# Loading the value weights in the order they are written, and giving the last quarter its own buffer

## The chip, the cores and the metric

The kernel runs on one core of one Trainium2 chip. The metric is the device time of one execution in microseconds. The five engines of a core have their own instruction queues and wait for each other only by semaphores: TensorE (PE) multiplies, VectorE (DVE), ScalarE (ACT) and GpSimd (POOL) work element by element, and SyncE (SP) only issues transfers between device memory and the on-chip memory. Each queue is worked off strictly in order.

## The reference

One step of a streaming encoder layer on 1024 prompt frames and 64 sample frames of width 1024. What matters here is its beginning: every frame is normalised by its root mean square, and the normalised frames are multiplied by one wide weight matrix that makes queries, keys, values, gates and more.

```python
def rmsnorm(x, g):
    xf = x.astype(jnp.float32)
    xf = xf * lax.rsqrt(jnp.mean(xf * xf, axis=-1, keepdims=True) + EPS)
    return (xf * g.astype(jnp.float32)).astype(x.dtype)

def project(x, g_norm, w_in, b_f):
    h = rmsnorm(x, g_norm) @ w_in
    q, k, v, gf, zf, u, gp, qm, gm = jnp.split(h, IN_SPLITS, axis=-1)
    logf = jax.nn.log_sigmoid(zf + b_f)
    ...
```

After that come causal attention with forget gates over 8 heads, attention to 256 memory tokens over 4 heads, a pooling mixer, a gated output projection, and a last normalisation. All of it is computed in float32 precision.

## The kernel before

**Arithmetic.** Each float32 operand of a large product is split into a high part (rounded to the fast matmul type) and a low part (the residue). A product is three matmuls: high by high, high by low, low by high. In the traces the high parts are `xh` and `whi`, the low parts `xl` and `wlo`. A high part is made by an ACT copy (or a DVE cast), a low part by one subtraction on DVE or POOL.

**The first stage.** The frames come in three chunks, `CH` (L30): frames 0 to 255 (x0), 256 to 767 (x1), 768 to 1087 (x2, with the 64 sample frames). `load_x` (L695) loads a chunk transposed, raw in `xr`, and splits it into `xh` and `xl`. The value weights come in four raw quarters called `wr`: `wv0` holds the first 256 value columns and the 8 forget columns, in two quarters of 4 k-slices each, and `wv1` the other 256 columns, in two quarters. `load_v` (L413) loads and splits one quarter. `load_w1` (L735) does so for `wv1`. All four raw quarters go through one ring of three buffers, so the fourth takes the buffer of the first.

**The statistics.** The root mean square of a frame comes from a second load of x, by frames instead of transposed: `load_r` (L720) calls `rstd` (L438), which loads blocks of 128 frames into `nat` (a ring of three buffers of 512 KB) and sums the squares, most blocks on ACT and the second block of a chunk on DVE. In the order, `nat_15`, `nat_16`, `nat_17` belong to x2, `nat_36`, `nat_37` to x0, and `nat_50` to `nat_53` to x1. The scale is applied only when a product leaves PSUM, from a small tile `rcol`.

**The value products.** `proj_v` (L724) computes, chunk by chunk, one PSUM accumulator per 128 frames and half of the columns. There are eight PSUM banks, two each of `pp`, `s`, `pt` and `o`. An accumulator's bank is free when its product has been scaled by `rcol` and copied out (`vr`, `zt`, and `vlo` for the sample frames, whose high and low halves are added first). The accumulators that the text speaks of: `s_31` (sample frames, second half of the columns), `s_42` (frames 128 to 255, first half; it takes the bank of `s_31`), `s_46` and `s_60` (which takes the bank of `s_46`), `s_48` (a transposition that spreads `rcol` over the partitions, in the bank of `s_42`).

**Afterwards** in the same stage: the cached keys are split and stored (`ck`, `hm`, `kd`), the 256 memory tokens are loaded (`memT`, `memn`, weights `wmk`, `wmv`, all through the `nat` ring) and projected, the forget gates are summed up, and the first query and key projections run with weights `wt` in the raw buffer of `load_w` (a single `wr` buffer in the pool `wp`). Attention and the output projection follow.

**What sets the order.** The program is written as plain calls, but `Planner` records each operation and emits all of them in an order of its own. `flush` (L200) steps through a model of the engines; when an engine is free, it takes the operation that can start first by the model; among those that can start at the same time, the lower `rank` wins, and then the longer remaining path (`level`). `add` (L89) sets the rank: -1 for operations that touch certain pools, else 0. Because the emitted queues are strict, the model's order holds on the chip even where its times do not. `WARM` (L29) is the number of throw-away matmuls at the very start.

**The transfers' slots.** The framework gives each transfer, in the order of issue, one of eight completion semaphores (`DMAHW0` to `DMAHW7` in the rows below). A transfer that is given a semaphore waits until the one that had it eight places before has landed. So eight transfers are under way at most, and SP stands still until the oldest lands. The very first semaphore goes to the small load of `gn_s`, which ACT issues.

## Time and profile before

| | |
|---|---|
| time, median of 3 runs | 590.33 us (590.27 to 591.16) |
| the profiled execution | 590.34 us, of which the profile's span is 588.5 us |
| PE busy | 561.2 us (95%) |
| DVE busy | 349.1 us (59%) |
| ACT busy | 299.1 us (51%) |
| POOL busy | 249.8 us (42%) |
| TensorE clock granted, mean | 0.996 |
| transfers | 126.33 MB, mean 215 GB/s |

How to read what follows. Times are microseconds from the start of the span. In a timeline row the first number is the start, the second the duration, then engine, line, operation, tiles, and in brackets how long the engine stood idle before it and what ended the idle time. In the table by windows, each engine has its busy time and its number of instructions in the stretch, and the last columns are the granted clock, the busy share of the 16 transfer engines and the GB/s. Nearly every instruction carries the line of the helper that emits it (L252), so rows are told apart by their tiles, whose numbers the profile leaves out. Rows of the emitted order carry the numbers. A busy PE in the table by windows counts the pipelined tail of a matmul too.

### The profile page before, as it was taken

The numbers are of one execution on the slowest core, as the hardware profiler recorded it, in microseconds if no ns is written. First come the engines' busy times: TensorE is split into PE (matmuls) and PEld (weight loads), VectorE is DVE, ScalarE is ACT, GpSimd is POOL, SyncE is SP. The second block draws the span as 40 slices with busy tenths as digits, with TensorE's granted clock in tenths as the row PEclk, the third lists the DMA queues.
The fourth block names the chain that finished last, engine by engine and source line by source line (L and its number), as shares of the span: only waits on it lengthen the run. The fifth ranks groups of instructions, "written<-read, shape, count | busy, mean of one in ns | idle before, by whom it ended". The sixth has DMA issues, their size and how long they took to land.

```text
span 588.5 us, 10778 instructions
## 1 busy us (share of the span) xinstructions
PE 561.2 (95%) x3623; PEld 504.3 (86%) x3623; DVE 349.1 (59%) x822; ACT 299.1 (51%) x675; POOL 249.8 (42%) x358
## 2 busy tenths in 40 slices
PE   7799999999999999999999999999999989999993
PEld 5789999888979889988988889889898867989983
DVE  5774431112788877756798965864356374656334
ACT  5564631121677877767886864862234243323202
POOL 2301464353774544434479851522323394322200
PEclk9999999999999999999999999999999999999998
DMA  8998753658997896596687897735256337577541
GB/s 301 312 339 298 229 174 117 242 202 281 281 349 242 291 280 189 154 322 210 213 238 269 274 263 235 210 125 152 76 152 187 113 109 195 142 231 213 159 143 72
DMA packets 96448, 126.33 MB, mean 215 GB/s; under 512 B 30434, under 2 KB 68618, under 8 KB 94858
## 3 DMA queue, kind: packets, MB, share of 16 engines
q1 hardware_dynamic: 96106, 125.39, 66.6%
q8 instruction: 29, 0.48, 0.3%
q10 hardware_dynamic: 288, 0.27, 0.1%
q14 instruction: 25, 0.20, 0.1%
HBM read 86.41 MB, written 39.21 MB: 213 GB/s over the span
## 4 chain that ended last, share of the span: by engine, by line
PE 76%; DMA 10%; DVE 6%; issue 3%; POOL 3%; ACT 1%; SPq 0%; DVEq 0%; POOLq 0%; ACTq 0%
PE pp L252 40%; PE s L252 13%; PE o L252 11%; PE pt L252 11%; DMA nat<-in_xn_dram 5%; POOL wl L252 2%; DMA nc<-gpd 2%; DMA nc<-gsd 1%; DMA catd<-cat 1%; DVE s L252 1%; DMA xr<-in_xT_dram 1%; DVE Q L252 1%; DVE ot L252 1%; DVE phl L252 1%; SPq L252 0%
## 5 line engine op out<-in xcount | busy, mean ns | idle before, releaser
L252 PE MATMUL pp<-xh,whi 128*128 128x320 f32 (+2 forms) x480 | 149.9, 335 | 2.8 <-DVE gr L252 1.1
L252 PE MATMUL pp<-xl,whi 128*128 128x320 f32 (+2 forms) x480 | 148.0, 331 | 0.0
L252 PE MATMUL pp<-xh,wlo 128*128 128x512 f32 (+2 forms) x480 | 147.7, 332 | 0.0
L252 PEld LDWEIGHTS pp<-xh,whi 128*128 128x128 f32 x480 | 88.1, 188 | 11.6 <-DVE gr L252 2.3
L252 POOL TENSOR_TENSOR wlo<-wr,whi 128x512 fp32r<-128x512 f32 (+2 forms) x44 | 60.1, 1384 | 86.7 <-ACT whi L252 75.1
L252 PEld LDWEIGHTS pp<-xh,wlo 128*128 128x128 f32 x480 | 88.1, 188 | 6.9
L252 PEld LDWEIGHTS pp<-xl,whi 128*128 128x128 f32 x480 | 88.1, 188 | 6.5
L252 DVE TENSOR_TENSOR phl<-pt,phl 128x512 fp32r<-128x512 f32 (+1 forms) x96 | 60.4, 642 | 11.9 <-ACT phl L252 10.8
L252 ACT CAST phl<-pt 128x512 fp32r<-128x512 f32 (+1 forms) x96 | 51.8, 550 | 25.0 <-PE pt L252 18.4
L252 POOL TENSOR_TENSOR cat<-ot 64x256 f32<-64x256 f32 x48 | 36.1, 754 | 55.6 <-DVE ot L252 33.0
L252 PE MATMUL o<-phl,vs 128*128 128x512 f32 (+1 forms) x160 | 55.3, 416 | 0.0
L252 PE MATMUL pt<-ident,Q 128*128 128x128 f32 x248 | 47.6, 272 | 1.9 <-DVE phl L252 1.8
L252 ACT CAST whi<-wr 128x1024 fp32r<-128x1024 f32 (+1 forms) x25 | 24.6, 982 | 45.2 <-PE pp L252 43.0
L252 ACT ACTIVATE Q<-Q,m 128x576 f32<-128x576 f32 (+4 forms) x40 | 38.0, 950 | 17.4 <-DVE m L252 17.1
L252 DVE TENSOR_TENSOR ot<-o,ot 64x512 f32<-64x512 f32 x48 | 32.8, 685 | 13.4 <-ACT ot L252 12.8
L252 PEld LDWEIGHTS pt<-ident,Q 128*128 128x128 f32 x248 | 32.1, 140 | 7.2 <-issue 2.2
L252 PE MATMUL s<-ks,qb 128*128 128x512 f32 (+3 forms) x128 | 37.4, 374 | 0.0
L252 POOL TENSOR_TENSOR P<-P,P 128x512 f32<-128x512 f32 (+2 forms) x17 | 18.5, 1096 | 41.8 <-DMA P<-catd 23.3
L252 ACT COPY ot<-o 64x512 f32<-64x512 f32 x48 | 27.9, 581 | 11.8 <-PE o L252 9.1
L252 PEld LDWEIGHTS o<-phl,vs 128*128 128x128 f32 x160 | 27.8, 190 | 3.3 <-DVE ot L252 0.2
L252 DVE CUSTOM_DVE_ANT_0 Q<-s,nc 128x512 f32<-128x512 f32 (+2 forms) x40 | 24.0, 599 | 10.9 <-PE s L252 6.0
L252 DVE TENSOR_TENSOR gr<-pp,rb 128x512 f32<-128x512 f32 (+2 forms) x24 | 12.5, 532 | 26.8 <-PE pp L252 25.8
(250 smaller groups left out, 1330.2 us busy)
## 6 DMA issues: line engine op xcount, KB each, us to landing
qd<-hl SPq DMA_DIRECT2D x24, 576.0 KB, 4.7
wr<-in_wt_dram SPq DMA_DIRECT2D x20, 512.0 KB, 4.2
qa<-qd SPq DMA_DIRECT2D x12, 640.0 KB, 5.7
ks<-kd SPq DMA_DIRECT2D x8, 800.0 KB, 6.4
qb<-qd SPq DMA_DIRECT2D x12, 512.0 KB, 5.0
P<-catd SPq DMA_DIRECT2D x17, 256.0 KB, 3.0
nat<-in_xn_dram SPq DMA_DIRECT2D x8, 512.0 KB, 8.1
kd<-hl SPq DMA_DIRECT2D x16, 256.0 KB, 5.1
```

The source lines that it names most:

```text
L252: getattr(getattr(self.nc, op.eng), op.fn)(*op.args, **op.kw)
```

## The change

Five edits, all in the first stage.

1. Operations recorded in `load_x(2)` get rank -3 on every engine but PE, those in `load_w1` rank -2 (`nc.first`); the transfers recorded in `load_x(0)` and `load_r(2)` get rank -1 (`nc.soon`). Where the planner's model has several operations ready at once, these go first, in the order in which they are written.
2. The fourth raw quarter of the value weights goes into the raw weight buffer of the projections (pool `wp`), which is later used for the `wt` weights. The first three keep the ring.
3. Three subtractions for low parts move from POOL to DVE: both pieces of the second quarter (128x528 each) and the third quarter (128x1024). The fourth quarter's stays on POOL.
4. `load_c` (the identity and `bf_s`) is called after these loads rather than between them.
5. One throw-away matmul less, 9 instead of 10.

```diff
-WARM = 10
+WARM = 9
...
         self.calm = self.boost = False
+        self.first = self.soon = 0
...
         op.rank = -1 if self.boost or urgent and not self.calm else 0
+        if self.first and eng != "tensor":
+            op.rank = -self.first
+        if self.soon and eng == "sync":
+            op.rank = -self.soon
...
     def load_v(g, a, wpool_, rpool, steps=(4,), hi_eng=None, lo_eng=None):
         gw = 264 if g == 0 else 256
-        raw = rpool.tile([P, WC], F32, tag="wr", name=nm("wr"), bufs=3)[:, : 4 * gw]
+        if rpool is wp:
+            raw = wp.tile([P, D], F32, tag="wr", name=nm("wr"), bufs=1)
+        else:
+            raw = rpool.tile([P, WC], F32, tag="wr", name=nm("wr"), bufs=3)[:, : 4 * gw]
...
-                        gen = load_v(0, a // 4, wp, xp, (2, 2), None, (nc.vector, nc.gpsimd)[a // 4])
+                        gen = load_v(0, a // 4, wp, xp, (2, 2), None, nc.vector)
...
             for a in (0, 1):
-                ws[1].append(next(load_v(1, a, xp, xp, (4,), (None, nc.vector)[a])))
-
+                ws[1].append(
+                    next(load_v(1, a, xp, (xp, wp)[a], (4,), (None, nc.vector)[a], (nc.vector, None)[a]))
+                )
+
+        nc.first = 3
         load_x(2)
-        load_c()
+        nc.first = 2
         load_w1()
+        nc.first = 0
+        nc.soon = 1
         load_x(0)
         load_r(2)
+        nc.soon = 0
+        load_c()
+
         proj_v(2)
```

The emitted order at three places follows; a row's bracket names the semaphores that it waits for. First, the transfers at the start of SP's queue, before the change (`xr2` is the raw x2, `wr_2` and `wr_5` the quarters of `wv0`):

```order
L252 DMA wr_125_267<-in_wt_dram 128x1024
L252 DMA nat_15_150<-in_xn_dram 128x1024
L252 DMA xr2_135<-in_xT_dram 128x2x320
L252 DMA wr_2_136<-in_wv0_dram 128x528
L252 DMA xr2_135<-in_xT_dram 128x2x320
L252 DMA wr_2_136<-in_wv0_dram 128x528
L252 DMA xr2_135<-in_xT_dram 128x2x320
L252 DMA wr_5_139<-in_wv0_dram 128x528 [waits DMAHW0_49]
L252 DMA xr2_135<-in_xT_dram 128x2x320 [waits DMAHW1_49]
L252 DMA wr_5_139<-in_wv0_dram 128x528 [waits DMAHW2_49]
```

And with the change:

```order
L257 DMA xr2_135<-in_xT_dram 128x2x320
L257 DMA wr_2_136<-in_wv0_dram 128x528
L257 DMA xr2_135<-in_xT_dram 128x2x320
L257 DMA wr_2_136<-in_wv0_dram 128x528
L257 DMA xr2_135<-in_xT_dram 128x2x320
L257 DMA wr_5_139<-in_wv0_dram 128x528
L257 DMA xr2_135<-in_xT_dram 128x2x320
L257 DMA wr_5_139<-in_wv0_dram 128x528 [waits DMAHW0_49]
L257 DMA wr_8_142<-in_wv1_dram 128x1024 [waits DMAHW1_49]
L257 DMA wr_11_145<-in_wv1_dram 128x1024 [waits DMAHW2_49]
L257 DMA nat_15_150<-in_xn_dram 128x1024 [waits DMAHW3_49]
```

The 512 KB of `wt` and the first statistics block no longer stand ahead of x2, and both quarters of `wv1` follow at once; `wt` is now the 31st transfer.

Second, further down SP's queue, the 23rd to the 32nd transfer, before the change (`xr1` is the raw x1, two transfers of 1 MB; the rows from `mask` to `winv` are small constants):

```order
L252 DMA mask_112<-in_mask_d_dram 128x128 [waits DMAHW7_49]
L252 DMA icnt_115<-in_icnt_d_dram 128x32 [waits DMAHW0_49]
L252 DMA psc_s_113<-in_psc_dram 128x2 [waits DMAHW1_49]
L252 DMA winv_114<-in_winv_d_dram 128x2 [waits DMAHW2_49]
L252 DMA wr_11_145<-in_wv1_dram 128x1024 [waits DMAHW3_49,DVE_49]
L252 DMA xr1_170<-in_xT_dram 128x4x512 [waits DMAHW4_49,DVE_49]
L252 DMA xr1_170<-in_xT_dram 128x4x512 [waits DMAHW5_49]
L252 DMA nat_50_186<-in_xn_dram 128x1024 [waits DMAHW6_49,Activation_49]
L252 DMA nat_37_173<-in_xn_dram 128x1024 [waits DMAHW7_49,DVE_49]
L252 DMA kd0_87<-hm_79_219 64x512 [waits DMAHW0_49,Activation_49]
```

And with the change, the same places:

```order
L257 DMA icnt_115<-in_icnt_d_dram 128x32 [waits DMAHW7_49]
L257 DMA psc_s_113<-in_psc_dram 128x2 [waits DMAHW0_49]
L257 DMA winv_114<-in_winv_d_dram 128x2 [waits DMAHW1_49]
L257 DMA xr1_170<-in_xT_dram 128x4x512 [waits DMAHW2_49,DVE_49]
L257 DMA xr1_170<-in_xT_dram 128x4x512 [waits DMAHW3_49]
L257 DMA nat_36_172<-in_xn_dram 128x1024 [waits DMAHW4_49,Activation_49]
L257 DMA nat_50_186<-in_xn_dram 128x1024 [waits DMAHW5_49,DVE_49]
L257 DMA nat_37_173<-in_xn_dram 128x1024 [waits DMAHW6_49,Activation_49]
L257 DMA wr_125_267<-in_wt_dram 128x1024 [waits DMAHW7_49,Pool_49]
L257 DMA kd0_87<-hm_79_219 64x512 [waits DMAHW0_49,Activation_49]
```

The last quarter of `wv1` has left this place, x1 follows the constants directly, and `nat_36`, which was the 19th transfer, now stands behind x1.

Third, on DVE, where the sum of the sample frames' halves, `vlo_32`, frees the bank of `s_31`, before the change (`ISA` is the sum of squares of a statistics block):

```order
L252 ISA nat_37_173,ss4_35_171<-nat_37_173 128x1024 [waits DMAHW7_49]
L252 ISA ss4_35_171 128x1
L252 TENSOR_SCALAR ms_38_174<-ss4_35_171 128x2 [waits DVE_49]
L252 RECIPROCAL rcol_120<-rt_39_175 128x2 [waits Activation_49]
L252 ISA nat_51_187,ss4_49_185<-nat_51_187 128x1024 [waits DMAHW2_49]
L252 ISA ss4_49_185 128x1
L252 TENSOR_TENSOR vlo_32_167<-s_31_166,vlo_32_167 64x256 [waits Activation_49]
```

And with the change:

```order
L257 ISA nat_37_173,ss4_35_171<-nat_37_173 128x1024 [waits DMAHW6_49]
L257 ISA ss4_35_171 128x1
L257 TENSOR_SCALAR ms_38_174<-ss4_35_171 128x2 [waits DVE_49,Activation_49]
L257 SCALAR_TENSOR_TENSOR xl1_128<-xr1_170,gn_s_107,xh1_125 128x512 [waits Activation_49]
L257 RECIPROCAL rcol_120<-rt_39_175 128x2 [waits Activation_49]
L257 TENSOR_TENSOR rcol_120<-rcol_120,ms_38_174 128x2 [waits DVE_49]
L257 TENSOR_TENSOR vlo_32_167<-s_31_166,vlo_32_167 64x256 [waits Activation_49]
```

`nat_51` no longer stands between `nat_37` and `vlo_32`; one split of x1 does. From about the sixth hundredth matmul on, and from the first query projections on the other engines, the emitted orders are the same.

## The prediction

> **What bounds the kernel now.** I first read the page's chain of work that ended last:
>
> ```profile
> PE 76%; DMA 10%; DVE 6%; issue 3%; POOL 3%; ACT 1%; SPq 0%; DVEq 0%; POOLq 0%; ACTq 0%
> ```
>
> PE bounds the program as a whole. The edits touch only the first stage, so I asked for the same chain in order of time:
>
> ```profile
> 1.69 5.16 DMA xr<-in_xT_dram
> 6.86 7.25 DMA nat<-in_xn_dram
> 14.20 8.07 DMA nat<-in_xn_dram
> ...
> 26.09 11.31 DMA nat<-in_xn_dram
> 37.42 1.23 DVE nat L252
> 39.04 3.42 PE s L252 x26
> ```
>
> Until 39 us it runs through transfers, not through PE: each is issued when the one eight places ahead has landed. The last link is a statistics block; PE takes over at 39.04. PE's waits in the first 100 us, and its work by stretches of 10 us, agree:
>
> ```profile
> PE o L252 <- ACT whi L252: 2.5, 1, 2.5
> PE s L252 <- ACT whi L252: 2.5, 1, 2.5
> PE s L252 <- DVE vlo L252: 1.5, 1, 1.5
> ```
>
> ```profile
> 10.00:20.00 10.00, 6.92 (x41) 6.51 (x40) 8.35 (x18) 7.10 (x15) 5.34 (x3) 1.00 1.07 331
> 30.00:40.00 10.00, 8.53 (x72) 8.33 (x71) 7.91 (x20) 5.91 (x12) 0.33 (x1) 1.00 0.95 333
> 40.00:50.00 10.00, 10.00 (x85) 10.00 (x84) 6.61 (x15) 6.00 (x15) 1.28 (x1) 1.00 0.99 346
> 50.00:60.00 10.00, 10.00 (x87) 10.00 (x86) 4.45 (x13) 3.82 (x9) 2.27 (x2) 1.00 0.76 249
> ```
>
> So before 39 us an earlier start of PE is worth nothing by itself: PE would only wait longer at the same gate. After it PE is full, 85 matmuls in 10 us, 0.12 us each. Two things count: when the gate opens, and how much PE has done by then.
>
> The gate is PE's first write into `s_42`. It needs the bank of `s_31`, which `vlo` on DVE frees. DVE and ACT around it:
>
> ```profile
> 35.17 1.23 DVE L252 CUSTOM_DVE_ANT_0 nat<-nat 128x1024 f32<-128x1024 f32 x1 [1.37 <-DMA nat<-in_xn_dram]
> 36.44 0.17 DVE L252 TENSOR_SCALAR ms<-ss 128x2 f32<-128x2 f32 x1
> 36.88 0.17 DVE L252 RECIPROCAL rcol<-rt 128x2 f32<-128x2 f32 x1 [0.27 <-ACT rt L252]
> 37.42 1.23 DVE L252 CUSTOM_DVE_ANT_0 nat<-nat 128x1024 f32<-128x1024 f32 x1 [0.38 <-DMA nat<-in_xn_dram]
> 38.57 0.41 DVE L252 TENSOR_TENSOR vlo<-s,vlo 64x256 f32<-64x256 f32 x1
> ```
>
> ```profile
> 28.80 2.57 ACT L252 ACTIVATE xh<-xr,gn_s 128x512 fp32r<-128x512 f32 x4 [3.74 <-DMA xr<-in_xT_dram]
> 32.56 1.34 ACT L252 ACTIVATE xh<-xr,gn_s 128x512 fp32r<-128x512 f32 x2 [1.19 <-DMA xr<-in_xT_dram]
> 36.64 0.20 ACT L252 ACTIVATE rt<-ms 128x2 f32<-128x2 f32 x1 [0.29 <-DVE ms L252]
> 36.87 0.37 ACT L252 COPY vlo<-s 64x256 f32<-64x256 f32 x1
> ```
>
> `nat_37` lands at 35.17; ACT's half of `vlo` ends at 37.24, 2.07 us later. DVE's half comes only at 38.57, because `nat_51` stands ahead of it and lands at 37.42.
>
> **The change part by part.**
>
> *The first loads.* x2 and `wv0` no longer stand behind `wt` and `nat_15`, 1 MB together. The first product may come up to 2.5 us earlier (PE's wait for the first `whi` in the list above). That is worth nothing, since PE then waits at the gate: the cover is the chain of transfers. If that cover were gone, these 2.5 us would be won in full.
>
> *When x1 is issued.* SP's queue between 20 and 24 us before:
>
> ```profile
> 20.07 0.33 SPq L252 DMA_DIRECT2D psc_s<-in_psc_dram  x1
> 20.75 0.33 SPq L252 DMA_DIRECT2D winv<-in_winv_d_dram  x1
> 22.33 0.33 SPq L252 DMA_DIRECT2D wr<-in_wv_dram  x1
> 22.75 0.93 SPq L252 DMA_DIRECT2D xr<-in_xT_dram  x2
> ```
>
> The first 18 transfers of both orders are the same set, except that the last quarter of `wv1` (512 KB) takes the place of `wt` (512 KB). So the 18th, `ck`, lands when it did: just before 20.75, since `winv`, eight places on, was issued then. Before, the next transfer waited for the 19th, `nat_36`, until 22.33. Now `nat_36` is no longer there. The first half of x1 waits for `ck` itself, behind `icnt`, `psc` and `winv`, which go out from about 20.07 at some 0.4 us each: **21.2 us**. The bounds are 20.75 (that issue alone) and 22.33 (nothing won).
>
> *When `nat_37` lands.* Before, from 22.33 on: a `wv1` quarter, x1, `nat_50`, `nat_37`, 3.5 MB, landed at 35.17, after 12.84 us. Now x1, `nat_36`, `nat_50`, `nat_37`, also 3.5 MB: 21.2 + 12.84 = **34.0**, with the bounds above 33.6 to 35.2.
>
> *When the gate opens.* From `nat_37` to the end of ACT's half 2.07 us as before: 36.1. On DVE a split of x1 now stands between; four took 2.7 us, so one takes 0.7:
>
> ```profile
> 31.07 2.73 DVE L252 SCALAR_TENSOR_TENSOR xl<-xr,gn_s,xh 128x512 fp32r<-128x512 f32 x4
> ```
>
> `ms` at 35.3, the split until 36.1, reciprocal and product 0.2 each, `vlo` 0.41: **36.9** instead of 39.04, 2.1 us earlier. ACT's two remaining copies of x1 end by 35.3 and don't decide.
>
> *What PE has done by then.* In the emitted order 185 matmuls of products stand ahead of the first one into `s_42` before the change, and 204 with it (8 more into `pt_29`, 25 more into the first accumulators of x1, 2 into `o_70`, against 16 fewer into x0's `pp` tiles). Nineteen more by 0.12 us: **2.3 us** that no longer come after the gate. PE can have them done: they need x1's second half (about 29.5 us by the rate above) and ACT's copies (35.3).
>
> *What is late next.* Two waits behind the gate are new. `s_60` needs `s_46` copied out by ACT, now behind the cast of a cached-key block, which by the queue lands near 37.2: the copy ends at 38.3, PE is there at 38.1, so 0.2 us. `s_48` needs `s_42` copied out, and ACT stands there behind the last two statistics blocks of x1. Before:
>
> ```profile
> 35.15 1.62 SPq L252 DMA_DIRECT2D nat<-in_xn_dram  x2
> 41.84 1.06 ACT L252 ACTIVATE nat<-nat 128x1024 f32<-128x1024 f32 x1 [0.58 <-DMA nat<-in_xn_dram]
> ```
>
> The second, issued at 36.4, landed at 41.8. Now it is issued when the key block has landed, about 37.3, and lands at 42.8; ACT sums it (1.06) and copies `s_42` until 44.4. PE is there after 59 matmuls, at 44.1. I take back 0.2 + 0.3 = **0.5 us**; the bounds are 0 and 2.
>
> *The subtractions on DVE* cost 2 x 0.71 + 1.23 us there and take 3.25 + 2.38 us from POOL:
>
> ```profile
> 8.22 0.71 DVE L252 TENSOR_TENSOR wlo<-wr,whi 128x528 fp32r<-128x528 f32 x1
> 11.43 3.25 POOL L252 TENSOR_TENSOR wlo<-wr,whi 128x528 fp32r<-128x528 f32 x2 [10.23 <-ACT whi L252]
> 17.91 2.38 POOL L252 TENSOR_TENSOR wlo<-wr,whi 128x1024 fp32r<-128x1024 f32 x1 [3.23 <-ACT whi L252]
> ```
>
> DVE is free for them before 16 us, and nothing of it reaches the gate. The fourth buffer costs `wt` a wait for the last subtraction, over by about 17 us; `wt` goes out near 24 and is used after 60. Both are put at nothing; without that cover DVE's 2.65 us would be the price.
>
> *One throw-away matmul* falls into the time before any data is there: nothing.
>
> *The sum:* 2.1 + 2.3 - 0.5 = **3.9 us**. It carries to the end if the rest stays led by PE: its order is the same, and it loads into buffers that PE's progress frees. The profiled execution took 590.34 us (its span 588.5), the median is 590.33: **586.4 us**.
>
> **The rivals.**
>
> *The gate opens earlier still.* If x1 comes at the lower bound and the `nat` blocks with it, PE is limited by x1's last copies on ACT at 35.3 and by its own work. The gate then opens near 35.4, 1.5 us more: 584.9. For it speaks that the 12.84 us contain some idle time of the transfer engines; against it, that `vlo` still follows `nat_37`.
>
> *The gain sticks in the statistics of x1.* If the block that `s_48` hangs on lands later than 42.8, PE waits one for one. At 46 us 3 us are given back and 589.5 us remain, no measurable change. For it: SP now issues three key stores and one key load ahead of it, each waiting for its slot. Against: the transfers keep their rate.
>
> *The memory section's loads become the bound*, and the kernel gets slower. The first token load went out at 38.68 before; its buffer is that of `nat_51`, which now lands near 40, and SP has seven more stores and loads ahead of it: I put it at 43.4, 4.7 us later. The slack there is ACT's idle time before it splits the memory weights:
>
> ```profile
> 62.35 1.05 ACT L252 CAST whi<-nat 128x1024 fp32r<-128x1024 f32 x1 [2.92 <-PE pp L252]
> 57.40 1.06 ACT L252 ACTIVATE nat<-nat 128x1024 f32<-128x1024 f32 x1 [5.61 <-DMA nat<-in_memn_dram]
> ```
>
> With 4.7 us of lateness through the whole chain and 2.9 of slack it would cost 1.8 us against before: 592.1. It decides once the memory weights are split later than PE now reaches them. Against it: the later tokens' loads shift by about 1 us only, and the new ACT order puts the first memory weight ahead of the 5.61 us wait.
>
> [...]
>
> *The planner's times are wrong in another way*, and `nat_37` lands at 35.2 as before: then the gate opens at 38.1 and 0.9 + 2.3 - 0.5 = 2.7 remain: 587.6.
>
> **How the numbers follow.** A change within 0.2% (1.2 us, to 589.1) can't be told from none. Chances: the forecast with its bounds and the late `nat_37`, 585.4 to 588, 0.53; the earlier gate 0.12; the clock 0.07; stuck in the statistics 0.15; the memory section 0.13. Faster is the first three and a little of the fourth, 0.74; the same 0.14; slower 0.12. The predicted time is 586.4. The range goes from 584.3 (the earlier gate) to 589.8 (the gain nearly gone), and leaves out the memory section and the far ends.
>
> **What would show it.** Right: the first x1 transfer issued near 21.2, `nat_37`'s sum on DVE starting near 34, the first `s` matmul after PE's long wait near 36.9, PE without gaps from 45 on, and the stretch after 100 us as before but 4 us earlier. Wrong: a PE wait of over 1 us between 38 and 75 us, above all for `s` on ACT (`vr`) or for `pt` and `s` on ACT or DVE (`whi`, `wlo`), or matmuls at 0.22 us after 15 us.

## The result, and the profile after the change

The changed kernel is slower: 592.31 us median (590.54 to 594.69) against 589.95 (587.43 to 591.70), a ratio of 1.0037 with an interval of 1.0023 to 1.0051. I forecast 586.4. The execution that was profiled is one of the faster ones, 590.89 us with a span of 589.1.

The same chain of waits that ends at 39 us before, now in order of time (start, duration, what):

```profile
24.84 10.24 DMA nat<-in_xn_dram
35.11 1.23 DVE nat L257
...
38.58 0.38 SPq L257
39.05 7.00 DMA nat<-in_xn_dram
...
47.22 0.37 ACT vr L257
47.64 0.43 PE s L257 x2
...
72.92 0.67 ACT whi L257
73.59 3.24 DMA out_dram<-vr
76.83 0.73 POOL hm L257
...
78.82 2.49 POOL wlo L257 x2
81.44 2.04 POOL tall L257 x14
```

Before, PE took the chain over at 39.04 and kept it until past 100 us, but for 1.5 us near 72. Now the chain leaves PE twice more: from 38.6 to 47.6 it runs through a statistics block of x1, and from 72.9 to 84 through ACT, DVE and POOL in the memory section. (The 3.24 us behind `out_dram` are the profile's guess of a releaser; no experiment below bears it out.)

PE's waits in the first 110 us, the largest and those of the memory section:

```profile
PE s L257 <- ACT vr L257: 1.9, 1, 1.9
...
PE pp L257 <- DVE wlo L257: 0.7, 1, 0.7
...
PE s L257 <- POOL tall L257: 0.5, 1, 0.5
...
PE pp L257 <- ACT whi L257: 0.3, 1, 0.3
```

And by stretches of 10 us, to be read beside the rows of before: 67 matmuls from 40 to 50 where there were 85.

```profile
40.00:50.00 10.00, 8.08 (x67) 7.76 (x66) 3.53 (x13) 3.37 (x7) 1.50 (x2) 1.00 0.94 327
```

The gate itself did open earlier. DVE:

```profile
35.11 1.23 DVE L257 CUSTOM_DVE_ANT_0 nat<-nat 128x1024 f32<-128x1024 f32 x1 [1.65 <-DMA nat<-in_xn_dram]
...
36.52 0.74 DVE L257 SCALAR_TENSOR_TENSOR xl<-xr,gn_s,xh 128x512 fp32r<-128x512 f32 x1
37.45 0.41 DVE L257 TENSOR_TENSOR vlo<-s,vlo 64x256 f32<-64x256 f32 x1
```

`vlo` ends at 37.86 and not 38.98, without the foreign block `nat_51` in front. PE now waits for another row there:

```profile
37.32 0.39 PE L257 MATMUL o<-whi,xl 128*128 128x264 f32 x1 [0.60 <-DVE xl L257]
...
38.03 0.28 PE L257 MATMUL s<-whi,xh 128*128 128x264 f32 x1
```

Its last wait is 0.60 us for the split `xl`, which DVE, too, does only behind the sum of `nat_37`; at `s_42`, the second row, it doesn't wait, because it gets there 0.17 us after `vlo`'s end. What comes behind the gate stands in SP's queue and on ACT:

```profile
22.65 0.93 SPq L257 DMA_DIRECT2D xr<-in_xT_dram  x2
...
32.56 2.98 SPq L257 DMA_DIRECT2D kd<-hm  x3
...
37.46 0.53 SPq L257 DMA_DIRECT2D nat<-in_xn_dram  x1
...
38.58 0.89 SPq L257 DMA_DIRECT2D nat<-in_xn_dram  x2
```

```profile
44.86 1.06 ACT L257 ACTIVATE nat<-nat 128x1024 f32<-128x1024 f32 x1 [5.40 <-DMA nat<-in_xn_dram]
46.07 1.06 ACT L257 ACTIVATE nat<-nat 128x1024 f32<-128x1024 f32 x1
47.13 0.46 ACT L257 ACTIVATE vr<-s,rcol 128x256 f32<-128x256 f32 x1
```

The two last blocks of x1 went out at 35.15 and 36.4 before. Now three key stores stand ahead of them, the blocks go out at 38.58 and 39.05, ACT sums them at 44.86 and 46.07 (40.12 and 41.84 before), and only then copies `s_42`, for which PE stands still.

**How much PE lost where.** Waits alone don't add up: from `s_42` to `s_48` the change has one listed wait of 1.9 us, and PE loses 2.54 there by the table below. So I counted the moving columns of all matmuls that the emitted order puts ahead of a landmark and multiplied them by 0.1204 us per 264 columns. That is close to the pace before the change, where the eleven steps from 13.70 to 15.04 us take 0.122 us each and the eleven from 39.75 to 41.07 us 0.120:

```profile
13.70 0.29 PE L252 MATMUL s<-whi,xh 128*128 128x264 f32 x1
13.83 0.28 PE L252 MATMUL pp<-wlo,xh 128*128 128x264 f32 x1
...
14.92 0.28 PE L252 MATMUL pp<-whi,xh 128*128 128x264 f32 x1
15.04 0.30 PE L252 MATMUL s<-whi,sx 128*128 128x264 f32 x1
```

PE's lag is the start of the landmark on the chip less this work; where it grows, PE lost that time. The landmarks: the first product into `s_42`; `s_48`; the spread of x1's `rcol`, called `s_72`; the spread of the memory's, `s_104`; and the first sum of the forget gates, the matmul on `tall`. The last two lines belong to experiments below.

| lag in us at | `s_42` | `s_48` | `s_72` | `s_104` | `tall` |
|---|---|---|---|---|---|
| before | 14.94 | 15.16 | 15.33 | 16.18 | 16.30 |
| the change | 11.91 | 14.45 | 14.78 | 16.58 | 17.50 |
| key stores later (e1) | 10.96 | 11.04 | 11.09 | 13.86 | 14.76 |
| memory section mended too (e16) | 11.61 | 11.69 | 11.75 | 12.21 | 12.40 |

The throw-away matmuls count as work in this table, and the change has one less, which is 0.23 us: in products alone its lead at the gate is 3.3 us.

By the table the change arrives at the gate 3.0 us ahead of before. It gives 2.3 back until `s_48`, and between `s_72` and `tall` it loses 2.72 where before lost 0.97: 1.75 more, which turns the lead into a deficit of 1.2 (1.0 in products alone). The rows at the end of this stretch, before:

```profile
77.67 0.38 PE L252 MATMUL s<-ident,rcol 128*128 128x128 f32 x2
85.85 0.50 PE L252 MATMUL s<-tall,onesm 128*128 128x200 f32 x2
104.39 1.09 DVE L252 TENSOR_TENSOR kr<-pp,rb 128x512 f32<-128x512 f32 x2 [8.13 <-PE pp L252]
```

and after:

```profile
74.96 0.39 PE L257 MATMUL pp<-whi,mhl 128*128 128x256 f32 x1 [0.31 <-ACT whi L257]
76.72 0.38 PE L257 MATMUL pp<-wlo,mhl 128*128 128x256 f32 x1 [0.67 <-DVE wlo L257]
77.84 0.43 PE L257 MATMUL s<-ident,rcol 128*128 128x128 f32 x2
84.24 0.61 PE L257 MATMUL s<-tall,onesm 128*128 128x200 f32 x2 [0.53 <-POOL tall L257]
105.45 1.09 DVE L257 TENSOR_TENSOR kr<-pp,rb 128x512 f32<-128x512 f32 x2 [8.17 <-PE pp L257]
```

(`tall` comes earlier after the change than before, yet PE has done 2.6 us less of products by then.) `kr`, the result of the first key projection, is 1.06 us late; what follows it takes 483.65 us instead of 484.11.

### The profile page after: what moved, and what is told of

The parts are those of the page before. It is cut to its first block, busy times and chain, and to the rows that moved or that the text cites. A ratio compares the mean times of both kernels' runs of the same rounds, so it can differ in the third digit from the quotient of the medians.

```text
span 589.1 us, 10781 instructions
## 1 busy us (share of the span) xinstructions
PE 561.0 (95%) x3622; PEld 502.4 (85%) x3622; DVE 348.1 (59%) x825; ACT 299.3 (51%) x675; POOL 247.2 (42%) x355
## 4 chain that ended last, share of the span: by engine, by line
PE 74%; DMA 9%; DVE 5%; POOL 4%; issue 4%; ACT 2%; SPq 1%; DVEq 0%; POOLq 0%; ACTq 0%
PE pp L257 40%; PE s L257 12%; PE o L257 11%; PE pt L257 11%; DMA nat<-in_xn_dram 3%; POOL wl L257 2%; DMA ck<-in_ckT_dram 2%; DMA nc<-gsd 1%; SPq L257 1%; DMA wr<-in_wv_dram 1%; DVE s L257 1%; DVE phl L257 1%; DMA catd<-cat 1%; DMA catd<-og 1%; DMA out_dram<-vr 1%
## 5 line engine op out<-in xcount | busy, mean ns | idle before, releaser
L257 PE MATMUL pp<-xh,whi 128*128 128x256 f32 (+2 forms) x480 | 149.9, 336 | 2.5 <-DVE gr L257 1.1
L257 POOL TENSOR_TENSOR wlo<-wr,whi 128x512 fp32r<-128x512 f32 (+1 forms) x41 | 55.5, 1374 | 76.9 <-ACT whi L257 58.2
L257 POOL TENSOR_TENSOR P<-P,P 128x512 f32<-128x512 f32 (+2 forms) x17 | 18.6, 1101 | 42.8 <-DMA P<-catd 28.0
```

The source lines that it names most:

```text
L257: getattr(getattr(self.nc, op.eng), op.fn)(*op.args, **op.kw)
```

## The experiments

The expectations speak of these theories. A: the key stores that now stand ahead of x1's last statistics in SP's queue. B: the subtractions moved to DVE. C: the throw-away matmul, and with it PE's clock. Later ones speak of the memory section: its loads come late, or its work stands in a worse order on ACT, DVE and POOL. All kernels compute everything. Except in e3, e4 and e11, where the planner orders anew, an emitted order is edited just before it is written out, so nothing but the named rows moves.

**The key stores, after the change (e1, e10).** The four stores of each cached-key block go out behind x1's last statistics, or behind the memory loads.

```diff
+        for source, after in (('hm_79', 'nat_52'), ('hm_81', 'nat_91'), ('hm_83', 'nat_95'), ('hm_85', 'nat_99')):
+            at = [o for o in done if o.eng == "sync" and (o.args[0].tensor.name + "_").startswith(after + "_")]
+            for op in [o for o in done if o.eng == "sync" and (o.args[1].tensor.name + "_").startswith(source + "_")]:
...
+                    done.insert(to, op)
```

> The changed kernel; on SP alone the stores of the cached keys (hm to kd) go out behind the statistics and memory-token loads instead of ahead of them. Nothing else moves. Theory A (the gain is lost because x1's last statistics blocks and the memory tokens' loads go out late, behind the key stores): PE's wait of 1.9 us for s on ACT vr near 46 us is gone, the last sum of x1's statistics ends near 43 instead of 47 us, the waits for whi, wlo and tall at 73 to 84 us shrink from 1.5 to under 0.5 us, and the time is 2 to 4 us under the changed kernel's, 588 to 590 us: ratio to before 0.995 to 0.999. Theory B (the subtractions moved to DVE cost it): no change against the changed kernel, ratio 1.003 to 1.004. Theory C (one throw-away matmul less, PE's clock): as B.

588.96 us against 590.08 (0.9973, 0.9957 to 0.9989), and a second time:

> The kernel of e1 once more, beside the others of this call, because the effects are of the size of the spread. If e1's gain is real: 588.9 and a ratio to the kernel before of 0.997 to 0.999; if it was luck, 590.

588.41 against 590.05 (0.9977, 0.9961 to 0.9994). SP and ACT of the first:

```profile
34.19 1.58 SPq L265 DMA_DIRECT2D nat<-in_xn_dram  x2
35.83 2.42 SPq L265 DMA_DIRECT2D kd<-hm  x4
```

```profile
41.12 1.06 ACT L265 ACTIVATE nat<-nat 128x1024 f32<-128x1024 f32 x1 [0.20 <-DMA nat<-in_xn_dram]
...
42.64 0.48 ACT L265 ACTIVATE vr<-s,rcol 128x256 f32<-128x256 f32 x1 [0.37 <-DVE zt L265]
```

The blocks go out 4.4 and 3.6 us earlier, PE's 1.9 us wait for `vr` is gone, and the lead of 4.0 us lasts until `s_72`. A is confirmed for that place. But only 1.1 to 1.6 us reach the end: the stretch to `tall` now takes 3.67 us more than its work (2.70 the second time). So there is a second loss, and it is not of SP's making alone.

**Only the first block's stores (e5).**

```diff
-        for source, after in (('hm_79', 'nat_52'), ('hm_81', 'nat_91'), ('hm_83', 'nat_95'), ('hm_85', 'nat_99')):
+        for source, after in (('hm_79', 'nat_52'),):
```

> The changed kernel; on SP alone the four stores of the first cached-key block go behind x1's last statistics blocks, but the stores of the second to fourth block stay where the change has them, ahead of the memory loads. e1 moved both groups and took 588.96 us, the changed kernel 592.31. If the late statistics of x1 alone cost the gain, this takes 589.0, the wait of 1.9 us for the copy of s_42 is gone and no new one comes. If the late memory loads alone cost it, it takes 592.3 and PE's waits for wlo, tall and whi after 60 us grow by what the wait at 47 us no longer takes. I expect something between, nearer to the first: 590.2, with the waits after 60 us at 2 to 3 us in all.

590.25 against 590.27 (1.0006, 0.9989 to 1.0023). It takes away the wait at `s_48` (lag 12.63, a lead of 2.5), and 3.55 us are lost behind `s_72`, as in e1. But in its profile the granted clock (last but two) halves from 30.9 to 34.3 us:

```profile
31.00:32.00 1.00, 1.00 (x6) 1.00 (x6) 1.00 (x2) 0.92 (x2) 0.00 (x0) 0.50 1.03 410
32.00:33.00 1.00, 1.00 (x7) 1.00 (x6) 1.00 (x3) 1.00 (x3) 0.00 (x0) 0.50 1.03 410
```

PE has no wait between 29.58 and the gate, which it reaches at 38.66, 0.6 us after `vlo`'s end and 1.6 later than in e1. So the smaller lead of this profile is not the stores': 0.6 us go with the clock, and `nat_37` came 1.1 later than in e1. By the medians, 590.25 against 588.96 and 588.41, the other three blocks' stores may be worth something of their own in e1; that isn't shown.

**The same move in the kernel before (e7).** Of the same lists' stores two stand ahead of x1's last statistics there, so two move.

> The control: the kernel before, with the same rule on SP (there it moves two stores of the first cached-key block behind x1's last statistics blocks, and nothing else). If e1's gain has nothing to do with the order of the first loads, and moving key stores is worth it in any order, this gains as much as e1: 589.0. If the gain is the earlier gate, kept only because the key stores no longer take it back, this stays at the kernel before, 590.1, or gains the 0.3 to 0.5 us by which nat_51, and with it vlo and the gate, comes earlier: 589.6.

591.50 against 590.27 (1.0029, 1.0010 to 1.0049), slower. The stores are not in the way there; moved back, they delay the memory tokens, which go out at 40.39 instead of 38.68 and are there 3.2 us later (44.55 before), and ACT's copy of `s_42` stands behind them:

```profile
47.78 1.71 ACT L260 ACTIVATE mhl<-nat,gm_s 128x256 fp32r<-128x256 f32 x4 [4.22 <-DMA nat<-in_memT_dram]
50.18 0.47 ACT L260 ACTIVATE vr<-s,rcol 128x256 f32<-128x256 f32 x1 [0.69 <-DVE zt L260]
```

A place in a queue is worth something only relative to the rest of the order.

**The edits one by one (e3, e4, e11) and two suspects (e2, e8).** Ranks and call order alone:

```diff
+        if self.first and eng != "tensor":
+            op.rank = -self.first
+        if self.soon and eng == "sync":
+            op.rank = -self.soon
...
+        nc.first = 3
         load_x(2)
...
```

> The kernel before with the ranks and the later load of the identity alone; the last quarter still shares the ring, the subtractions stay on POOL, ten throw-away matmuls. Its order has nat_51 as 40th transfer and the first memory tokens as 50th, as late as in the changed kernel. Theory A: slower than before by 1 to 3 us, ratio 1.002 to 1.005. Theories B and C: not slower, ratio under 1.001.

592.52 against 590.08 (1.0038, 1.0021 to 1.0055). The fourth buffer alone:

```diff
-                ws[1].append(next(load_v(1, a, xp, xp, (4,), (None, nc.vector)[a])))
+                ws[1].append(next(load_v(1, a, xp, (xp, wp)[a], (4,), (None, nc.vector)[a])))
```

> The kernel before with the last quarter in the projections' raw buffer alone. Its order has nat_51 as 32nd transfer and the first memory tokens as 43rd, as early as before. Theory A: as before within 1.5 us, ratio 0.998 to 1.002. Theories B and C say the same, since neither of their edits is in it; if it is slower, none of the three holds and the buffer itself costs.

593.01 against 590.08 (1.0051, 1.0034 to 1.0068). The subtractions alone:

```diff
-                        gen = load_v(0, a // 4, wp, xp, (2, 2), None, (nc.vector, nc.gpsimd)[a // 4])
+                        gen = load_v(0, a // 4, wp, xp, (2, 2), None, nc.vector)
```

> The kernel before with edit 3 alone: the three subtractions on DVE. The planner orders everything anew. By theory B (DVE becomes the bound at the start) it is slower, 592; by theory A it is as before when its order keeps x1's last statistics blocks ahead of the key stores, 590.1. Edits 1 with 4 alone and edit 2 alone were both slower by 2.4 to 2.9 us, so I give slower the better chance here too: 591.5. What tells it is the lag of PE at the first x1 product, at the spread of rcol and at the tall row, each against the kernel before.

591.11 against 590.05 (1.0024, 1.0008 to 1.0039). Each is slower by itself, by 2.4, 2.9 and 1.1 us; together they cost 2.4. They are no terms of a sum, because each makes the planner put the whole stage in another order: the wait at the gate is 3.0 us in e4, and e3 and e11 have gaps of their own (in e3 the largest are 3.3 us in two waits for `sx`). The profiles of all three also have a stretch at half the clock (last section).

The changed kernel with the second and third quarter's subtractions back on POOL, in the same order otherwise:

```diff
+            if op.fn == "tensor_tensor" and op.eng == "vector" and any(op.args[0].tensor.name.startswith(n) for n in ("wlo_7", "wlo_10")):
+                op.eng = "gpsimd"
```

> The changed kernel in its emitted order, except that the subtractions of the second and the third quarter run on POOL again, as before the change. Theory A: as the changed kernel, ratio 1.003 to 1.004, with the same waits (s on ACT vr near 46 us). Theory B: back to before or better, ratio under 1.001. Theory C: as A.

590.80 against 590.08 (1.0014, 0.9995 to 1.0033). It has the same waits (`vr` 1.7, `wlo` 0.7, `tall` 0.5), and its profile loses 3.04 us between `s_72` and `tall`. As the whole cause B finds no support; whether the 1.5 us to the changed kernel are in part real, this doesn't tell. And with ten throw-away matmuls:

```diff
-WARM = 9
+WARM = 10
```

> The changed kernel with ten throw-away matmuls again instead of nine; every order else is that of the change. If the missing one cost PE's clock (theory C), it takes 590.6 or less. If, as I expect, the key stores on SP cost the gain and this edit is worth nothing, it takes 592.3, and its profile is a second look at the changed order: first x1 transfer near 22.6, the wait for the copy of s_42 1 to 2 us, and waits of 2 us in all for whi, wlo and tall after 60 us.

591.97 against 590.27 (1.0024, 1.0006 to 1.0041): as slow as the change without this edit. C falls.

**What is slow in the memory section (e6, e9, e12, e14).** First the order of the two halves of the memory's value weights, on top of e1: on ACT both casts ahead of a copy-out (`vr_67`) and the first half first, on DVE the same, and POOL's subtraction for the next weights (`wlo_137`, 2.54 us) behind the `tall` rows. The first half came first before the change too, but POOL's subtraction stood ahead of most `tall` rows there as well (at 79.24).

```diff
+        for eng, what, where, anchor in [('scalar', ('whi_115', 'nat_114'), 'before', ('vr_67', 'pp_66')),
+                ('scalar', ('whi_112', 'nat_111'), 'before', ('whi_115', 'nat_114')),
+                ('vector', ('wlo_113', 'nat_111'), 'before', ('wlo_116', 'nat_114')),
+                ('gpsimd', ('wlo_137', 'wr_135'), 'before', ('hm_109', 'mkr_108'))]:
```

> e1 with three rows moved in the memory section: ACT casts the first half of the memory value weights ahead of the second half (PE needs them in that order) and both ahead of one copy of a projection, DVE subtracts the first half first, and POOL's subtraction of the second wt block goes behind the last forget-gate row (tall). In e1 PE waits there 0.3 us for whi, 0.6 for wlo and 0.5 for tall. If the conversions of the memory section now hold PE, and not its own work, these three waits go and it takes 588.96 - 1.4 = 587.6. If PE only meets the next wait, it takes 589.0 as e1.

589.81 against 590.27 (0.9993, 0.9980 to 1.0006). The waits for `wlo` and `tall` are gone, and 2.93 us are lost all the same: PE now waits 1.05 us for `rcol` at 75.56. Then the second token block (`nat_100`) first in SP's queue, so that its sum comes earlier:

```diff
+        for op in [o for o in done if o.eng == "sync" and named(o, "nat_100")]:
+            done.remove(op)
+            done.insert(max(i for i, o in enumerate(done) if op in o.succ) + 1, op)
```

> e6 with one more row moved, on SP: the load of the second block of memory tokens goes ahead of the first-issued half of the memory value weights, which there waits for another buffer (61.9 us in e1, 60.7 expected here). In e6 PE waited 1.0 us for rcol, which hangs on the sum of that block (DVE, 67.56). If the loads of the memory section hold PE, the sum starts 1.2 to 2.5 us earlier, the wait for rcol goes, and the time falls by about 1 us below e6 and below e1: 588.0. If PE is held by something else in that stretch, the wait goes to another name and the time stays at that of e1.

587.80 against 590.05 (0.9967, 0.9950 to 0.9984), faster than before, though in its profile the stretch still loses 3.23. On top of that all token and weight loads between 51 and 66 us ahead of key stores and result stores:

```diff
+        for ahead, behind in [('nat_99', 'vr_61'), ('nat_99', 'vr_65'), ('nat_99', 'hm_83'), ('nat_111', 'vr_59'),
+                ('nat_111', 'hm_87'), ('nat_111', 'vr_45'), ('nat_111', 'vr_71'), ('nat_111', 'vr_41'), ('nat_114', 'hm_85')]:
```

> e9 with SP's rows between 51 and 66 us in another order and nothing else: the first block of memory tokens directly behind the second key weights (its buffer is free at 53.7 in e1, it is issued at 56.1 there), the second block, then both halves of the memory value weights directly behind them, and the key stores of the third and fourth block and the stores of results after these. PE's work from the spread of rcol near 51 us to the tall row near 82 us takes 0.97 us more than its matmuls alone in the kernel before (2.72 in the changed kernel, 3.67 in e1, 3.23 in e9). If it is the loads of the memory section that hold PE there, the first sum on ACT starts 2 us earlier against PE, the casts of the value weights 1 to 1.5 us earlier, the loss falls to 2 us or less and the time to 586.8. If it is the order in which PE itself, ACT and DVE are emitted, the loss stays at 2.7 or more and the time at 587.8 to 588.9.

589.09 against 590.34 (0.9987, 0.9970 to 1.0003), and the loss is 2.85. Both token blocks go out earlier (53.56 and 60.39 us; 56.11 and 61.91 in e1) and nothing is won: late token loads are not what holds PE there. The half of the value weights that is cast first still goes out second, at 64.40 (64.07 in e1), and ACT waits 2.1 us for it ahead of the casts at 70.19, so that load isn't ruled out. Last a single row on top of e1, the cast of the second key weights (`whi_96`) ahead of ACT's sum of a token block (`nat_99`). The change has put this sum between the casts of the two key weights; before, it stood ahead of both:

```diff
+        for eng, what, where, anchor in [('scalar', ('whi_96', 'nat_95'), 'before', ('nat_99', 'ss4_98'))]:
```

> e1 with the first of these two moves alone: on ACT the cast of the second key weights ahead of the sum of the first token block. If that row's place sets when the value weights can be loaded (their buffer is freed by the subtraction behind this cast), their load goes out 0.8 to 1.0 us earlier than in e1 (64.1 us there, with s_48 at 44.2), PE's waits for whi and wlo, 0.3 and 0.6, go, the wait for tall stays, and the time is 588.2. If not, 588.9 as e1.

588.57 against 590.50 (0.9965, 0.9950 to 0.9979); loss 2.73, as in e10. This row alone doesn't do it.

**The chain as a whole (e13, e15, e16, e17).** What is left is a chain through several engines: ACT casts a weight when PE has freed its buffer, sums a token block behind it, takes the root (`rt_102`) behind the casts of the value weights, DVE makes `rcol` from it, and only then can PE spread it. Here `whi_96` goes ahead of the sum, and the root and the four small DVE operations of `rcol` ahead of the casts, on top of e12:

```diff
+        for eng, what, where, anchor in [('scalar', ('whi_96', 'nat_95'), 'before', ('nat_99', 'ss4_98')),
+                ('scalar', ('rt_102', 'ms_101'), 'before', ('whi_112', 'nat_111'))]:
...
+            done[at:at] = ms + rt + ops
```

> e12 with two rows moved on ACT and their followers on DVE: the cast of the second key weights goes ahead of the sum of the first token block (in the kernel before it stood there too, as ACT's first free row), and the square root for the tokens, with the four small rcol rows behind it on DVE, ahead of the casts of the value weights. In all kernels with the change's order PE loses 2.7 to 3.7 us between the spread of rcol near 51 us and the tall row, in all with the order of before 1.0 to 1.2, and e12 shows that earlier loads alone don't alter it (2.85). If the cause is the emitted chain on ACT and DVE from the weight buffer that PE frees to the value weights, 1.1 us longer by that sum and closed by the rcol rows, the loss falls to 1.5 us, the waits for rcol and whi go, and the time is 587.8. If the chain is not the cause, the loss stays at 2.7 or more and the time at 589.0.

590.80 against 590.50 (1.0007, 0.9992 to 1.0023), a miss: the loss is 4.6 us. Part of it is of my own making: `vr_67`, which e6 had put behind the casts, now holds PE. Right behind this wait the clock is at half in this profile, from 74.76 to 78.18: products of 256 columns start 0.21 us apart there, and 0.12 apart near 71 and 79 us.

```profile
74.25 0.39 PE L320 MATMUL pp<-whi,mhl 128*128 128x256 f32 x1 [2.51 <-ACT vr L320]
```

With `vr_67` ahead of the casts again, and the last key stores behind the value weights' loads:

```diff
+        for ahead, behind in [("vr_45", "hm_85")]:
...
+        for eng, what, where, anchor in [('scalar', ('vr_67', 'pp_66'), 'before', ('whi_112', 'nat_111'))]:
```

> e13 with its own fault taken out: in e13 a copy of a projection stood on ACT behind the casts of the value weights, and PE waited 2.5 us for it. Here that copy goes first, and on SP the stores of the fourth key block go behind the second half of the value weights, which was issued late in e13 (65.9 against 64.1 us in e1). If the emitted chain on ACT and DVE is what costs PE 2.7 to 3.7 us between the spread of rcol and the tall row, the loss now falls to 1.7 us or less, no wait above 0.5 us is left there, and the time is 587.5. If the loss stays at 2.7 or more again, PE's own order (12 products of the first key projection fewer ahead of the tall row than before, 2.8 us of work) is what is left as its cause, and the time is 588.5 to 590.

588.49 against 590.46 (0.9976, 0.9957 to 0.9995), and the stretch from `s_72` to `tall` takes 0.66 us more than its work, less than the 0.97 before the change. The half of the value weights that is cast first now goes out at 62.39. PE's own order is that of e12, which lost 2.85, so it isn't the cause. Behind the stretch my earlier move has left one wait: POOL's subtraction stands ahead of the `zall` copies that follow `tall`.

```profile
81.83 0.61 PE L342 MATMUL s<-zall,tri 128*128 128x200 f32 x2 [1.57 <-POOL zall L342]
```

So the subtraction goes behind those as well:

```diff
+        for eng, what, where, anchor in [('gpsimd', ('wlo_137', 'wr_135'), 'before', ('hm_106', 'mkr_105'))]:
```

> e15 with POOL's subtraction of the second wt block moved once more, behind the four copies of zall that e15 leaves late (in e15's profile the loss between the spread of rcol and the tall row was 0.66 us, as the chain theory said, but the subtraction of 2.53 us that had been put behind the tall rows then stood ahead of zall, and PE waited 1.6 us for it at 81.8). If that was the last wait of the memory section, the kr row comes 1.4 us earlier against the spread of rcol than in e15 (51.4 us there, 50.1 in the kernel before after taking out the 3.9 us of other work that it does in between), and the time is 587.2, below e1 and e10. If another wait follows, 588.5 as e15.

**587.18 us against 590.27** (0.9943, 0.9922 to 0.9964), eight executions. And once more, with six:

> The kernel of e16 once more, with more executions. If its gain is real, 587.2 again, 2.5 to 3.1 us below the kernel before; if the eight executions of e16 were lucky ones, 588.5 as e15.

**586.29 against 590.20** (0.9939, 0.9918 to 0.9961). PE and the subtraction in the first of the two:

```profile
73.47 0.38 PE L354 MATMUL s<-ident,rcol 128*128 128x128 f32 x2
79.14 0.50 PE L354 MATMUL s<-tall,onesm 128*128 128x200 f32 x2
81.08 0.61 PE L354 MATMUL s<-zall,tri 128*128 128x200 f32 x2
```

```profile
80.98 2.54 POOL L354 TENSOR_TENSOR wlo<-wr,whi 128x512 fp32r<-128x512 f32 x2
```

```profile
100.58 1.09 DVE L354 TENSOR_TENSOR kr<-pp,rb 128x512 f32<-128x512 f32 x2 [8.24 <-PE pp L354]
```

No wait stands at these three PE rows, and the subtraction begins when PE is past `tall`. `kr` comes 3.8 us earlier than before (99.84, 4.6 us earlier, in the second), and the two medians are 3.1 and 3.9 us below before. This is the change with its two losses taken out, and it beats both kernels. Whether the new order of the memory section would also help the kernel before wasn't tried, nor was it separated how much of it is due to the root, the cast, the loads and the last key stores each. Some of these places are new to both kernels: before the change, too, the root stands behind the casts of the value weights and POOL's subtraction ahead of most `tall` rows. So the cause lies in the order on ACT, DVE, POOL and SP, but which of the rows that the change moved costs the 1.75 us isn't shown.

**The change again (e18):**

> The changed kernel once more, beside e16's. Its profiled execution was 1.4 us below its median; with a second profile it can be seen whether the two take-backs (2.3 us at the copy of s_42, 1.8 us up to the tall row) are larger in another execution. I expect 592.2, a wait of 1.7 to 2.5 us for the copy of s_42, and a loss of 2.7 to 3.2 us up to the tall row.

592.68 against 590.20 (1.0040, 1.0022 to 1.0057). Its profile (592.92, span 591.1) has the first one's waits, another of 0.6 us at `s_72`, a loss of 2.82 up to `tall`, and `kr` at 106.22.

## Why the prediction was wrong, by its steps

- **First loads, buffer, throw-away matmul at nothing.** That nothing of the start reaches the end by itself is right for the throw-away matmul (e8). The rest can't be priced alone, since e3, e4 and e11 run in other orders.
- **When x1 is issued: 21.2.** It was 22.65, beyond my bound of 22.33. The 18th transfer, `ck`, did not land where it did before. Its eighth successor went out at 20.75 before (`winv`) and at 22.65 now (the first half of x1). `ck` itself was issued at 13.14 instead of 12.28 and took 9.4 us instead of about 8.5. I had taken the same set of transfers to mean the same landing time.
- **`nat_37` at 34.0.** 35.11 in the profile of the change, 34.01 to 36.17 over the experiments that keep its order up to there. The forecast is the lower edge of this scatter: 34.01, 34.04 and 34.07 did occur, the middle is 35.1.
- **The gate at 36.9 instead of 39.04.** In the change `vlo` ends at 37.86 and the first product starts at 38.03, 1.0 us earlier instead of 2.1. The step from `nat_37` to `vlo` is right: in e1, where `nat_37` came at 34.15, `vlo` ended at 36.91. Not right is that ACT's last copies of x1 end by 35.3 and don't decide. They ended at 36.28 (two statistics blocks stand ahead of them), PE waited 0.57 us for them and 0.60 for the split behind `nat_37`, and reached the gate just behind `vlo`. So the gate opened about when PE came, and a still earlier `vlo` alone would have won nothing.
- **More work done: 2.3 us.** Counted by columns 2.26, and it was done. Together the lead at the gate was 3.3 us in products of a predicted 4.4, and 4.2 in e1.
- **What is late next: 0.5 us, bounds 0 and 2.** This is the first step that failed, by its size: 2.3 us. The mechanism was named (ACT stands behind x1's last blocks, SP issues key stores ahead of them), but I put the second block's issue at 37.3 and its landing at 42.8, since a key block was to land at 37.2. It went out at 39.05 and was summed from 46.07 on. The three stores took SP from 32.56 to 35.54, each waiting for a slot that a statistics block still held (2.4 us in three waits); the result store behind them waited 1.2 us for the slot of `wt`; and from 37.46 on SP issued one row after the other. I had counted one wait, for the key block, where every row ahead waits for a slot of its own. The transfer then took 7.0 us and not the 5.5 that I had assumed. e1 shows the stores' part by taking them away: issue at 35.45, sum at 41.12. This is the rival "stuck in the statistics" with most of its price.
- **"It carries to the end if the rest stays led by PE: its order is the same."** This is the second step that failed, and the larger mistake, because behind the gate only the lateness of the loads was checked (in a rival), not the order of the engines. PE's order there is much the same (26.73 us of work between `s_72` and `tall` before, 27.79 with the change); that of ACT, DVE and POOL is not. It costs 1.75 us more than before even with the small lead that was left, and 2.7 to 3.7 where the lead arrives (e1, e10, e5): a lead at the entrance is lost there until the chain is mended (0.66, 0.65, 0.64 in e15 to e17). Which of the moved rows cost it stays open, as said above.
- **The rivals.** "The memory section becomes the bound" named the place and, with 592.1, almost the time, but by another mechanism: it was to be late token loads, and e12, with the token loads earlier, still loses 2.85. I had even counted ACT's new order there as speaking against it. The chance for the clock, 0.07, was one for a slow pace of PE after 15 us, with matmuls 0.22 us apart as from 9.37 to 13.55 us before the change (the granted clock reads 1.00 there). The trace of before has no matmul at that pace after 15 us, so the chance rested on no measured cause and no measured price. It cost nothing that shows in the two profiles of the change: the first has no such stretch before 583 us, and in the second the clock is at half from 21.9 to 25.3 us, ahead of the gate. In e4, e5 and e13 half the clock did cost time (last section). The earlier gate didn't come.
- **The sum of 3.9.** e16 and e17 deliver about as much (3.1 and 3.9), but that doesn't confirm its terms: their memory section also loses 0.3 us less than that of the kernel before, which the sum doesn't have. So most of the gain was there, and the change as it stands gives it back in two places: 3.0 at the gate, less 2.3, less 0.2 until `s_72`, less 1.75, makes -1.2 at `tall`, or -1.0 without the throw-away matmul, which fits the 1.06 us of `kr`.

What stays open: between the two profiles of before and after lie 0.6 us, between the medians 2.4. The second profile of the change explains part of that with a later `kr` (1.8 us instead of 1.1), and 484.9 us behind it instead of 484.1. Executions of one kernel scatter by about 2 us to either side, and why the changed kernel's profiled execution was a mild one isn't known.

## What to carry to other kernels

A gain at a gate is worth what the next queues let through: follow it, engine by engine, to the first place where PE was just in time before, and read the order of the engines PE waits for, not only PE's own. Where a planner sets the order, one edit re-orders all that follows, so edits tried one by one do not add up, and the losses are found by moving rows of the emitted order. Comparing PE's lag (start less emitted work) at a few landmarks shows where a lead is lost even where no single wait is long.

## What the runs showed of the hardware

**A half-speed clock in the middle.** In e4, PE waits 3.0 us at the gate, and 1.5 us after it goes on, the granted clock (last but two) halves:

```profile
40.00:41.00 1.00, 1.00 (x10) 1.00 (x9) 1.00 (x4) 0.48 (x1) 1.00 (x1) 0.97 1.08 410
41.00:42.00 1.00, 1.00 (x7) 1.00 (x6) 0.82 (x1) 0.00 (x0) 0.27 (x1) 0.50 0.97 363
...
43.00:44.00 1.00, 1.00 (x6) 1.00 (x6) 0.00 (x0) 0.93 (x3) 0.00 (x0) 0.50 1.00 306
44.00:45.00 1.00, 1.00 (x9) 1.00 (x9) 0.00 (x0) 1.00 (x2) 0.00 (x0) 0.82 1.07 377
```

From the shares 0.97 and 0.82 it lasts from 40.94 to 44.36, 3.4 us, at 6 to 7 matmuls per us instead of 10 to 11 (0.22 us apart from 41.48 on, 0.12 from 39.68 to 40.88): some 1.7 us lost (PE's lag grows by 1.8 us from `s_42` to `s_48` there, by 0.2 before the change). In the 3.4 us ahead of the drop PE was idle for 1.9 (its wait ended at 39.45). Nine other experiments (e3, e5, e7, e10, e11, e13, e14, e16, e18) show such drops ahead of the last 15 us. Most last 3.4 us again; the one in e3 and the second in e11 last 6.8. In the 3.4 us ahead of the drop PE was idle for 1.7 us in e10 and e14, 1.8 in e11 (the second), 1.9 in e18, 2.0 in e16 and 2.5 in e13. What starts such a stretch isn't shown: the wait of 2.5 us before the change (15.34 to 17.88) had none behind it.

What it costs depends on where it falls. In e7, e14, e16 and e18 it lies before 28 us and PE waits again behind it; the fast e16 is one of them. In e5 (30.9 to 34.3) and e11 (31.6 to 38.4) PE has no further wait between the slow stretch and the gate, and in e13 it lies in the memory section. e3 (13.6 to 20.5) and e10 (23.7 to 27.2) have mean clocks of 0.986 and 0.989, lower than these stretches explain: 0.990 and 0.993, an estimate from the 0.996 of before, less half of 6.8 and 3.4 us in 590. What makes the difference wasn't looked into.

**A sum on DVE and subtractions on POOL that meet.** The sum of a token block on DVE and POOL's pair of subtractions, apart (before):

```profile
68.19 1.22 DVE L252 CUSTOM_DVE_ANT_0 nat<-nat 128x1024 f32<-128x1024 f32 x1 [0.82 <-DMA nat<-in_memn_dram]
```

```profile
69.89 2.55 POOL L252 TENSOR_TENSOR wlo<-wr,whi 128x512 fp32r<-128x512 f32 x2 [2.13 <-ACT whi L252]
```

and at the same time (after):

```profile
69.37 2.14 DVE L257 CUSTOM_DVE_ANT_0 nat<-nat 128x1024 f32<-128x1024 f32 x1 [2.52 <-DMA nat<-in_memn_dram]
```

```profile
69.14 3.52 POOL L257 TENSOR_TENSOR wlo<-wr,whi 128x512 fp32r<-128x512 f32 x2 [1.50 <-ACT whi L257]
```

Each takes 0.9 to 1.0 us longer: 2.14 instead of 1.22 us on DVE, 3.52 instead of 2.55 on POOL. In e1 they overlap too (1.73 and 3.53 us), in e16 they stand apart (1.23 and 2.54). How the one holds up the other isn't shown. In the memory section of these four profiles, the orders that let the two meet lengthened both.
